# Block sums on VectorE, the first gate/up pair's weight operands kept in HBM, and the output stores spread over the last product

## Chip, core and metric

One NeuronCore of a Trainium2 chip runs the whole kernel. The metric is the device time of one execution in microseconds (us); the time before is the median of three executions.

## What is computed

A decoder layer over 1024 prompt tokens and 8 sample tokens, all fp32. The part that the change touches is its second half, and the gates ahead of it:

```python
h = rms_norm(x, norm1);  z = h @ w_in                # pool, q, k, v, ga, gb
merged = sigmoid(ga) * (y_pool @ w_pool_proj) + sigmoid(gb) * (y_attn @ w_attn_proj)
x = x + merged @ w_out
h2 = rms_norm(x, norm2)
x = x + (silu(h2 @ w_gate) * (h2 @ w_up)) @ w_down   # D_FF = 2816
```

## The kernel before

Every fp32 product is made of three fp32r products: each operand is split into a high part (a cast on ACT, line 138 for weights, 212 for activations) and the rest (a subtraction on DVE, lines 139 and 213), and PE adds high by high, high by rest and rest by high (`triple`, lines 1082 to 1086; `mm`, 207 to 209). All 1032 tokens are columns in two streams of 516, each of two halves of 258. A high part and a rest take a slot of the pools `whi` and `wlo` (4 slots each); raw weight blocks of 256 KB take one of 3 slots of `wraw`.

The stages in order of time, with the trace's times of before:

- attention and projections, to about 350 us;
- gates, 352 to 451: eight times `gate(1280, m)` with 72 matmuls, the first four followed by `mix(m)`;
- pool projection, 452 to 497;
- `out_proj(s, m)`, 497 to about 600: for stream s and block m 48 matmuls, the residual, a store of it to the HBM scratch `x2scr`, its square on ACT and a running sum of squares `acc` on POOL (line 969);
- for each stream `norm_scale` (the second RMS norm) and `combos`, which forms the seven left operands of a Strassen product from the four quarters of the normalized stream: four sums on POOL (lines 1011 to 1020), seven splits on ACT and DVE;
- gate and up products, about 597 to 1066: passes n = 0 to 11 over pairs p of 256 columns. Pass 0 is pair 0 for stream 0 alone, passes 1 to 10 are pairs 1 to 10 for both streams, pass 11 is pair 0 for stream 1. So stream 1 can still be normalized while pass 0 runs. `strassen` makes seven products for w_gate and seven for w_up; `wblocks` loads four quarters of a weight in two 512 KB transfers (`raw`), forms four differences on DVE (lines 1070 to 1078) and splits seven operands. Pair 0 is loaded and formed twice, in passes 0 and 11. A product is 12 matmuls where one stream runs and 24 where both do;
- `save` forms sums of a pass's result on POOL (line 1171, four per pass) and stores seven of them to HBM scratch (`s`);
- down products dx(1), dx(2), dy(6), dy(7), dy(4), dz(5), dz(3), 1066 to 1308. They read `ar` from that scratch and blocks `H` and `d` of w_down; `d`'s temporaries are slots of `wraw`. After dx(1), 12 additions `y` run on POOL. `residuals` loads 16 tiles `y` of 258 KB from `x2scr`;
- `store` (line 1293): five transposes on PE into one PSUM bank `po`, two copies on ACT (`ob` 128x512, `ys`), two or three transfers out. Sixteen of them; most are called where j == 3 of the last product.

The matmuls have one engine to themselves, PE. The order on each engine is made by a scheduler that models times, so it can move instructions across the order in which they are written. All transfers named here are issued by SP, one queue in order: a transfer that waits for a free slot holds all behind it.

Of the kernel before, what the change touches and what calls it, by code (L numbers as in the profile page):

```python
# [16 lines left out]
P = 128  # L17
# [19 lines left out]
def hybrid_step(tc, x_prompt, x_sample, cache_k, cache_v, state_pool, norm1, w_in, q_norm, k_norm, sinks,  # L37
# [860 lines left out]
    for what, m in ORDER:  # L898
        if what == "e":
            with tc.issue_after(live[15].yv.ins):  # L900
                pool_means(m)
        elif what == "g":
            attn_gate(m)
        elif what == "b":
            attn_proj(m)
    sg = []
    for m in range(8):
        sg.append(unit(u1, f"sg{m}"))
        gate(1280, m, sg[m])
        if m < 4:  # L910
            mix(m)
# [41 lines left out]
    def out_proj(s, m):  # L953
        ws = wload(wo_v, 0, 8, P * m)
        x2 = wide("x2")[:, :HT].rearrange("p (t c) -> p t c", t=2)
        xs = xscr[:, m].rearrange("p (t q c) -> p t q c", t=2, q=2)[:, :, s]
        SP.dma_start(x2, xs)
        ps = dbank("pw")
        for t in range(2):
            mm(ps[:, t, :NQ], ws, lambda k: (Mh[k][:, quarter(t, s)], Ml[k][:, quarter(t, s)]))  # L960
        V.tensor_add(x2, ps[:, :, :NQ], x2)
        SP.dma_start(x2scr[:, m, :, s], x2)
        if m == 0:
            A.activation(acc[s], x2, AF.Square)
        else:
            sq = t516("sq2").rearrange("p (t c) -> p t c", t=2)
            A.activation(sq, x2, AF.Square)  # L967
            if m < 7:
                G.tensor_add(acc[s], acc[s], sq)  # L969
            else:  # L970
                last[s] = sq
        A.activation(XG[s][:, :, m], x2, AF.Copy, scale=g2[m])
# [27 lines left out]
    def combos(s, out):  # L1000
# [10 lines left out]
        G.tensor_add(s1, a21, a22)  # L1011
        parts(1, a11)
        yield
        G.tensor_sub(s2, s1, a11)
        parts(2, a12)
        yield
        G.tensor_sub(a21, a11, a21)
        parts(6, s2)
        yield
        G.tensor_sub(a12, a12, s2)  # L1020
# [67 lines left out]
    def strassen(view, c0, streams, out):  # L1088

        sl = slice(streams[0], streams[-1] + 1)  # L1090
        ws = wblocks(view, c0)
# [73 lines left out]
    def save(p, g, sl):  # L1165
# [10 lines left out]
        comb(G.tensor_add, s1, a21, a22)  # L1176
        put(4, a22)
        put(5, s1)
        comb(G.tensor_sub, s2, s1, a11)
        put(6, s2)  # L1180
        comb(G.tensor_sub, a21, a11, a21)
        put(7, a21)
        put(2, a12)
        comb(G.tensor_sub, s4, a12, s2)
# [3 lines left out]
    norm = chain(norm_scale(1), combos(1, hc[1]))  # L1188
    for n, (p, streams) in enumerate([(0, [0])] + [(p, [0, 1]) for p in range(1, 11)] + [(0, [1])]):
        g = Gate()  # L1190
        u_ = Up(g)
        for i, _ in enumerate(chain(strassen(wg_v, 2 * P * p, streams, g), strassen(wu_v, 2 * P * p, streams, u_))):
# [33 lines left out]

    H1, H2 = {}, {}
# [7 lines left out]
    def operand(i, kk):  # L1235
# [3 lines left out]
        if i == 2:  # L1239
            return wd_row(k1, 0, wtemp("d21"))  # L1240
        if i == 6:
            w = wd_row(k0, 1, wtemp("d12"))
# [6 lines left out]
        if i == 4:  # L1249
            w = wd_row(k1, 0, wtemp("d21"))  # L1250
            V.tensor_sub(w, w, H1[kk])
            return w
        if i == 5:
            w = wtemp("t1")
# [38 lines left out]
    def store(f, t, y):  # L1293
# [10 lines left out]
        A.copy(o2[:n, :P], po[:n, 1, 0:P])  # L1304
# [15 lines left out]
    def residuals():  # L1320
        m1_es.close()
        mw_es.close()
        md, es = pool("md", bufs=20, side="right")
        mt[0] = md
        for t, m in ((0, 1), (1, 1), (1, 0), (0, 0)):
            Y[t, m] = residual(t, m)
# [31 lines left out]
    def stores(j, full=True):  # L1358
        for t, m, yy in ((0, 0, y11), (1, 0, y21), (1, 1, y22)) if full else ((0, 1, y12),):
            store(4 * m + j, t, yy[j])  # L1360

    for j in J:
        if j:
            stores(j - 1, False)
        if j == 2:
            stores(0)
        if j == 3:
            stores(1)
            stores(2)
            stores(3)  # L1370
        for kg in range(3):
# [7 lines left out]
            for k in range(n):  # L1379
                kk = 4 * kg + k  # L1380
                ah, al = a[kk]
                for s in range(2):
                    triple(z[j][:, s, :NQ], wh[:, k], wl[:, k], ah[:, s], al[:, s], False, kk == 10)
        V.tensor_add(y12[j], z[j][:, :, :NQ], y12[j])
    stores(3, False)
# [29 lines left out]
```

## Time and profile before

| | |
|---|---|
| median of 3 runs | 1323.27 us (1323.01 to 1325.38) |
| the profiled execution | 1322.94 us |
| its span in the trace | 1321.1 us |
| PE, PEld | 97%, 94% of the span |
| DVE, ACT, POOL | 63%, 38%, 15% |
| mean granted TensorE clock | 0.987 |
| HBM read, written | 105.10 MB, 34.48 MB |

The profile's page gives busy shares of the whole span. The trace behind it can be asked for single stretches: busy time by window, waits by engine, instructions by line and shape, the chain of work that ended last. A granted clock of 1.00 is the full 2.4 GHz, 0.50 the lower level; values between are stretches that hold both.

### The profile page before, as it was taken

The page shows a single profiled execution, that of the slowest core. Times are in us where ns is not written, and L with a number is a line of the kernel's source. Part 1 is how long each engine was busy: PE and PEld are TensorE (multiplying, and loading weights), DVE is VectorE, ACT ScalarE, POOL GpSimd, SP SyncE. Part 2 cuts the span into 40 slices and gives each one's busy share as a digit, 9 for nine tenths or more (in the row PEclk, how much of TensorE's full clock was granted, in tenths as well). Part 3 has the DMA queues.
Part 4 walks back from the last instruction along what each step waited for, and adds up shares of the span by engine and source line. Part 5 has one row for each costly group of instructions (what it writes and reads, how often), then busy time and mean ns, then how long its engine had stood idle before and what let it go on. Part 6 is the DMA issues. An engine that isn't in the chain of part 4 may idle for free.

```text
span 1321.1 us, 23770 instructions
## 1 busy us (share of the span) xinstructions
PE 1275.6 (97%) x9436; PEld 1243.5 (94%) x9436; DVE 838.8 (63%) x1519; ACT 507.8 (38%) x1003; POOL 195.1 (15%) x271
## 2 busy tenths in 40 slices
PE   7999999999999999987899999999999899899996
PEld 6998888999999999987899999999999899899996
DVE  6768667576233483499766567666666866766840
ACT  6555445442132234455323233222332343344423
POOL 3213200100000001152321022220122216000000
PEclk9999999999999999998899999999999999999998
DMA  7411101212111125643232222322323656855304
GB/s 243 136 35 41 41 21 44 77 36 57 41 49 48 49 81 156 173 126 106 77 121 77 93 97 98 121 89 81 113 81 121 209 192 217 263 182 194 121 9 121
DMA packets 139518, 139.86 MB, mean 106 GB/s; under 512 B 14391, under 2 KB 112375, under 8 KB 139383
## 3 DMA queue, kind: packets, MB, share of 16 engines
q1 hardware_dynamic: 139311, 137.08, 33.2%
q8 instruction: 74, 1.21, 0.4%
q0 software_dynamic: 96, 1.27, 0.2%
q14 instruction: 37, 0.30, 0.1%
HBM read 105.10 MB, written 34.48 MB: 106 GB/s over the span
## 4 chain that ended last, share of the span: by engine, by line
PE 89%; DVE 4%; DMA 3%; issue 2%; SPq 1%; ACT 1%; POOL 0%; DVEq 0%; ACTq 0%
PE pg L207 5%; PE pg L208 5%; PE pg L209 5%; PE py L1084 5%; PE py L1085 4%; PE py L1086 4%; PE pz L1086 3%; PE px L1084 3%; PE pz L1084 3%; PE px L1086 3%; PE pz L1085 3%; PE px L1085 3%; PE dy L1086 2%; PE dy L1084 2%; PE dy L1085 2%; PE pw L209 2%
## 5 line engine op out<-in xcount | busy, mean ns | idle before, releaser
L138 ACT CAST whi<-t 128x512 fp32r<-128x512 f32 x107 | 66.1, 621 | 174.9 <-PE py L1085 78.2
L207 PE MATMUL pg<-hTh,whi 128*128 128x384 f32 (+1 forms) x384 | 123.4, 322 | 0.0
L208 PE MATMUL pg<-hTl,whi 128*128 128x384 f32 (+1 forms) x384 | 123.1, 321 | 0.0
L209 PE MATMUL pg<-hTh,wlo 128*128 128x384 f32 (+1 forms) x384 | 122.7, 320 | 0.0
L139 DVE TENSOR_TENSOR wlo<-wraw,whi 128x512 fp32r<-128x512 f32 x95 | 70.2, 739 | 64.1 <-ACT whi L138 64.0
L138 ACT CAST whi<-wraw 128x512 fp32r<-128x512 f32 x95 | 58.8, 620 | 122.7 <-PE pa L208 31.3
L138 ACT CAST whi<-raw 128x512 fp32r<-128x512 f32 x72 | 44.5, 620 | 128.7 <-PE px L1085 49.0
L139 DVE TENSOR_TENSOR wlo<-t,whi 128x512 fp32r<-128x512 f32 x107 | 84.2, 789 | 14.6 <-ACT whi L138 14.3
L1171 POOL TENSOR_TENSOR fs<-g,g 128x516 f32<-128x516 f32 (+1 forms) x12 | 24.0, 2004 | 365.5 <-DVE g L1163 365.5
L209 PE MATMUL pw<-mh,wlo 128*128 128x258 f32 x256 | 73.1, 286 | 3.4 <-DVE wlo L139 3.4
L1084 PE MATMUL dy<-ah,whi 128*128 128x258 f32 x264 | 74.3, 284 | 0.6 <-DVE y L1339 0.6
L1085 PE MATMUL dy<-al,whi 128*128 128x258 f32 x264 | 74.0, 283 | 0.0
L212 ACT CAST ah<-ar 128x1032 fp32r<-128x1032 f32 (+1 forms) x42 | 41.3, 983 | 84.2 <-DMA ar<-s 77.9
L213 DVE TENSOR_TENSOR al<-ar,ah 128x1032 fp32r<-128x1032 f32 (+1 forms) x42 | 52.3, 1245 | 33.3 <-ACT ah L212 32.2
L207 PEld LDWEIGHTS pg<-hTh,whi 128*128 128x128 f32 x384 | 72.2, 188 | 1.1 <-DVE t L820 0.2
L207 PE MATMUL pw<-mh,whi 128*128 128x258 f32 x256 | 73.0, 285 | 0.0
L208 PEld LDWEIGHTS pg<-hTl,whi 128*128 128x128 f32 x384 | 72.2, 188 | 0.9
L208 PE MATMUL pw<-ml,whi 128*128 128x258 f32 x256 | 72.7, 284 | 0.0
L209 PEld LDWEIGHTS pg<-hTh,wlo 128*128 128x128 f32 x384 | 72.0, 188 | 0.4
L1086 PE MATMUL dy<-ah,wlo 128*128 128x258 f32 x264 | 72.0, 283 | 0.0
L969 POOL TENSOR_TENSOR acc<-acc,sq 128x516 f32<-128x516 f32 x12 | 17.4, 1446 | 315.1 <-ACT sq L967 315.1
L1084 PE MATMUL py<-c6h,whi 128*128 128x258 f32 x176 | 50.8, 289 | 6.2 <-DVE g L1160 6.2
(399 smaller groups left out, 4619.1 us busy)
## 6 DMA issues: line engine op xcount, KB each, us to landing
ar<-s SPq DMA_DIRECT2D x35, 516.0 KB
raw<-in_w_gate_dram SPq DMA_DIRECT2D x24, 512.0 KB
raw<-in_w_up_dram SPq DMA_DIRECT2D x24, 512.0 KB
s<-g SPq DMA_DIRECT2D x40, 258.0 KB
wraw<-in_w_in_dram SPq DMA_DIRECT2D x40, 256.0 KB
H<-in_w_down_dram SPq DMA_DIRECT2D x33, 256.0 KB
d<-in_w_down_dram SPq DMA_DIRECT2D x33, 256.0 KB
wraw<-in_w_out_dram SPq DMA_DIRECT2D x32, 256.0 KB
```

What stands on the lines that cost most here:

```text
L138: A.copy(hi, raw)
L139: e.tensor_sub(lo, raw, hi.bitcast(F32))
L207: T.matmul(ps, lhsT=wh, rhs=xh, start=(k == 0), stop=False)
L208: T.matmul(ps, lhsT=wh, rhs=xl, start=False, stop=False)
L209: T.matmul(ps, lhsT=wl, rhs=xh, start=False, stop=(k == n - 1))
L212: A.copy(hi, src)
L213: e.tensor_sub(lo, src, hi.bitcast(F32))
L969: G.tensor_add(acc[s], acc[s], sq)
L1084: T.matmul(ps, lhsT=wh, rhs=ah, start=start, stop=False, skip_group_check=True)
L1085: T.matmul(ps, lhsT=wh, rhs=al, start=False, stop=False, skip_group_check=True)
L1086: T.matmul(ps, lhsT=wl, rhs=ah, start=False, stop=stop, skip_group_check=True)
L1171: op(o[:, sl], a[:, sl], b[:, sl])
```

## The change

1. The running sums of squares (line 969), the sums in `combos` (1011 to 1020) and those in `save` (1171) move from POOL (`G`) to DVE (`V`): 12, 8 and 48 instructions.
2. `first_pair()` forms the 14 split operands of pair 0 during the gates, two per `gate` call for m = 0 to 6: 8 loads of 256 KB into `wraw`, 8 differences on DVE, 14 splits, and 28 stores of 256 KB to a new HBM scratch `wscr` (7.3 MB).
3. `kept()` gives those operands to passes 0 and 11: pass 0 reads 28 transfers of 256 KB straight into `whi`/`wlo` slots, pass 11 reads 14 of 512 KB into large units `wk`. Loads, differences and splits of pair 0 go from both passes (per pass 4 loads of 512 KB, 8 differences, 14 casts, 14 subtractions).
4. `dtemp`: the temporaries of w_down get four slots of their own (`wd`) in the pool `md`, which has 18 tiles in place of 20.
5. `store`: the copy `ys` goes from ACT to DVE; 15 of the 16 stores are called inside the last product, one after every second block for j = 1 to 3, and one is left for after it.

```diff
--- before.py
+++ after.py
@@ -903,10 +903,50 @@
             attn_gate(m)
         elif what == "b":
             attn_proj(m)
+
+    wscr = [scr.tile([P, 2, 4, P], F32, name=f"w{i}") for i in range(14)]
+
+    def first_pair():
+        for o, view in ((0, wg_v), (7, wu_v)):
+            def load(kh, m):
+                w = wraw()
+                SP.dma_start(w, view[:, 4 * kh:4 * kh + 4, P * m:P * m + P])
+                return w
+
+            def keep(i, w):
+                for a, part in enumerate(wsplit(w, 4)):
+                    SP.dma_start(wscr[o + i][:, a], part.bitcast(F32))
+
+            w = load(0, 0)
+            keep(0, w)
+            yield
+            b12 = load(0, 1)
+            V.tensor_sub(w, b12, w)
+            keep(4, w)
+            yield
+            b22 = load(1, 1)
+            keep(6, b22)
+            yield
+            V.tensor_sub(b12, b22, b12)
+            keep(3, b12)
+            yield
+            V.tensor_sub(w, b22, w)
+            keep(1, w)
+            yield
+            b21 = load(1, 0)
+            keep(2, b21)
+            yield
+            V.tensor_sub(w, b21, w)
+            keep(5, w)
+            yield
+
+    pre = first_pair()
     sg = []
     for m in range(8):
         sg.append(unit(u1, f"sg{m}"))
         gate(1280, m, sg[m])
+        for _ in range(2):
+            next(pre, None)
         if m < 4:
             mix(m)
     Mh, Ml = [], []
@@ -966,7 +1006,7 @@
             sq = t516("sq2").rearrange("p (t c) -> p t c", t=2)
             A.activation(sq, x2, AF.Square)
             if m < 7:
-                G.tensor_add(acc[s], acc[s], sq)
+                V.tensor_add(acc[s], acc[s], sq)
             else:
                 last[s] = sq
         A.activation(XG[s][:, :, m], x2, AF.Copy, scale=g2[m])
@@ -1008,16 +1048,16 @@
             out[i] = [x.rearrange("p (k c) -> p k c", k=4) for x in (hi, lo)]
 
         s1, s2 = unit(u1, "s1"), unit(u1, "s2")
-        G.tensor_add(s1, a21, a22)
+        V.tensor_add(s1, a21, a22)
         parts(1, a11)
         yield
-        G.tensor_sub(s2, s1, a11)
+        V.tensor_sub(s2, s1, a11)
         parts(2, a12)
         yield
-        G.tensor_sub(a21, a11, a21)
+        V.tensor_sub(a21, a11, a21)
         parts(6, s2)
         yield
-        G.tensor_sub(a12, a12, s2)
+        V.tensor_sub(a12, a12, s2)
         parts(7, a21)
         yield
         parts(5, s1)
@@ -1085,10 +1125,9 @@
         T.matmul(ps, lhsT=wh, rhs=al, start=False, stop=False, skip_group_check=True)
         T.matmul(ps, lhsT=wl, rhs=ah, start=False, stop=stop, skip_group_check=True)
 
-    def strassen(view, c0, streams, out):
+    def strassen(ws, streams, out):
 
         sl = slice(streams[0], streams[-1] + 1)
-        ws = wblocks(view, c0)
 
         def bank(name):
             return dbank(name)[:, sl, :NQ]
@@ -1173,23 +1212,38 @@
         a11, a12, a21, a22 = g[0, 0], g[0, 1], g[1, 0], g[1, 1]
         put(1, a11)
         s1, s2, s4 = half("fs1"), half("fs2"), half("fs4")
-        comb(G.tensor_add, s1, a21, a22)
+        comb(V.tensor_add, s1, a21, a22)
         put(4, a22)
         put(5, s1)
-        comb(G.tensor_sub, s2, s1, a11)
+        comb(V.tensor_sub, s2, s1, a11)
         put(6, s2)
-        comb(G.tensor_sub, a21, a11, a21)
+        comb(V.tensor_sub, a21, a11, a21)
         put(7, a21)
         put(2, a12)
-        comb(G.tensor_sub, s4, a12, s2)
+        comb(V.tensor_sub, s4, a12, s2)
         put(3, s4)
 
 
     norm = chain(norm_scale(1), combos(1, hc[1]))
+    def kept(o, in_units):
+
+        for i in range(7):
+            if in_units:
+                u = unit(u1, "wk", F32R)
+                SP.dma_start(u[:, :1024].bitcast(F32), wscr[o + i].rearrange("p a k c -> p (a k c)"))
+                u = u[:, :1024].rearrange("p (a k c) -> p a k c", a=2, k=4)
+                yield u[:, 0], u[:, 1]
+            else:
+                r = [wp.tile([P, 4, P], F32R, tag=t, bufs=4, name=t) for t in ("whi", "wlo")]
+                for a in range(2):
+                    SP.dma_start(r[a].bitcast(F32), wscr[o + i][:, a])
+                yield r
+
     for n, (p, streams) in enumerate([(0, [0])] + [(p, [0, 1]) for p in range(1, 11)] + [(0, [1])]):
         g = Gate()
         u_ = Up(g)
-        for i, _ in enumerate(chain(strassen(wg_v, 2 * P * p, streams, g), strassen(wu_v, 2 * P * p, streams, u_))):
+        for i, _ in enumerate(chain(strassen(wblocks(wg_v, 2 * P * p) if p else kept(0, n), streams, g),
+                                    strassen(wblocks(wu_v, 2 * P * p) if p else kept(7, n), streams, u_))):
             if n == 0 and i in (1, 4, 5, 6, 7, 8, 9, 10, 11):
                 next(norm)
         if n == 0:
@@ -1224,6 +1278,9 @@
         SP.dma_start(dst.rearrange("p j c -> p (j c)"), wd_v[:, f, 512 * m:512 * m + 512])
         return dst
 
+    def dtemp(name):
+        return Y["w"].tile([P, 4, P], F32, tag="wd", bufs=4, name=name)
+
     H1, H2 = {}, {}
 
     def keep(h, kk):
@@ -1237,9 +1294,9 @@
         if i == 1:
             return wd_row(k0, 0, keep(H1, kk))
         if i == 2:
-            return wd_row(k1, 0, wtemp("d21"))
+            return wd_row(k1, 0, dtemp("d21"))
         if i == 6:
-            w = wd_row(k0, 1, wtemp("d12"))
+            w = wd_row(k0, 1, dtemp("d12"))
             h2 = wd_row(k1, 1, keep(H2, kk))
             V.tensor_sub(h2, h2, w)
             V.tensor_add(H1[kk], H1[kk], h2)
@@ -1247,11 +1304,11 @@
         if i == 7:
             return H2[kk]
         if i == 4:
-            w = wd_row(k1, 0, wtemp("d21"))
+            w = wd_row(k1, 0, dtemp("d21"))
             V.tensor_sub(w, w, H1[kk])
             return w
         if i == 5:
-            w = wtemp("t1")
+            w = dtemp("t1")
             wd_row(k1, 1, H2[kk])
             V.tensor_sub(w, H2[kk], H1[kk])
             return w
@@ -1301,7 +1358,7 @@
         T.transpose(po[:n, 1, 0:P], y[:, small], ident)
         ob, o2 = t512("ob3"), t512("ys")
         A.copy(ob, po[:, 0])
-        A.copy(o2[:n, :P], po[:n, 1, 0:P])
+        V.tensor_copy(o2[:n, :P], po[:n, 1, 0:P])
         cols_ = slice(P * f, P * f + P)
         if t == 0:
             SP.dma_start(y_sample[:, 0, cols_], o2[:NS, :P])
@@ -1320,8 +1377,9 @@
     def residuals():
         m1_es.close()
         mw_es.close()
-        md, es = pool("md", bufs=20, side="right")
+        md, es = pool("md", bufs=18, side="right")
         mt[0] = md
+        Y["w"] = md
         for t, m in ((0, 1), (1, 1), (1, 0), (0, 0)):
             Y[t, m] = residual(t, m)
         Y["es"] = es
@@ -1355,19 +1413,14 @@
     for _ in srcs(3, a):
         pass
 
-    def stores(j, full=True):
-        for t, m, yy in ((0, 0, y11), (1, 0, y21), (1, 1, y22)) if full else ((0, 1, y12),):
-            store(4 * m + j, t, yy[j])
-
+    def full(j):
+        return [(4 * m + j, t, yy[j]) for t, m, yy in ((0, 0, y11), (1, 0, y21), (1, 1, y22))]
+
+    def part(j):
+        return [(4 + j, 0, y12[j])]
+
+    todo = full(0) + full(1) + part(0) + full(2) + part(1) + full(3) + part(2)
     for j in J:
-        if j:
-            stores(j - 1, False)
-        if j == 2:
-            stores(0)
-        if j == 3:
-            stores(1)
-            stores(2)
-            stores(3)
         for kg in range(3):
             n = min(4, 11 - 4 * kg)
             wh, wl = (wp.tile([P, 4, P], F32R, tag=t, bufs=4, name=t) for t in ("whi", "wlo"))
@@ -1381,8 +1434,10 @@
                 ah, al = a[kk]
                 for s in range(2):
                     triple(z[j][:, s, :NQ], wh[:, k], wl[:, k], ah[:, s], al[:, s], False, kk == 10)
+                if j and kk % 2:
+                    store(*todo.pop(0))
         V.tensor_add(y12[j], z[j][:, :, :NQ], y12[j])
-    stores(3, False)
+    store(*part(3)[0])
     flush()
     for e in (Y["es"], pd_es, u1_es, scr_es, tmp_es, wp_es, const_es):
         e.close()
```

The order that results, on SP. In the gates stage (before, where `wraw` are the raw slots):

```order
L692 DMA out_dram<-ob 8x128
L151 DMA wraw<-in_w_in_dram 128x4x128
L198 DMA wraw<-in_w_attn_proj_dram 64x4x128 x4
L151 DMA wraw<-in_w_in_dram 128x4x128 x16
L151 DMA wraw<-in_w_pool_proj_dram 128x4x128 x8
```

and now (`w_4181` and so on are the blocks of `wscr`):

```order
L151 DMA wraw<-in_w_in_dram 128x4x128 x2
L913 DMA wraw<-in_w_gate_dram 128x4x128 x2
L151 DMA wraw<-in_w_in_dram 128x4x128
L918 DMA w_4181<-whi 128x512
L918 DMA w_4181<-wlo 128x512
L918 DMA w_4185<-whi 128x512
L918 DMA w_4185<-wlo 128x512
L151 DMA wraw<-in_w_in_dram 128x4x128
L913 DMA wraw<-in_w_gate_dram 128x4x128
L918 DMA w_4187<-whi 128x512
L918 DMA w_4187<-wlo 128x512
L151 DMA wraw<-in_w_in_dram 128x4x128
```

The run of sixteen loads is broken up: loads of `w_in` now stand behind stores that wait for a cast on ACT or a subtraction on DVE.

From the last tiles of `out_proj` into pass 0, before:

```order
L1066 DMA raw<-in_w_gate_dram 128x4x256
L962 DMA x2scr<-x_6498 128x2x258
L1066 DMA raw<-in_w_gate_dram 128x4x256
L962 DMA x2scr<-x_6576 128x2x258
L1066 DMA raw<-in_w_up_dram 128x4x256 x2
L962 DMA x2scr<-x_6649 128x2x258
```

and now:

```order
L1106 DMA raw<-in_w_gate_dram 128x4x256
L1239 DMA whi<-w_4181 128x512
L1239 DMA wlo<-w_4181 128x512
L1239 DMA whi<-w_4182 128x512
L1239 DMA wlo<-w_4182 128x512
L1002 DMA x2scr<-x_6620 128x2x258
L1239 DMA whi<-w_4183 128x512
L1239 DMA wlo<-w_4183 128x512
L1106 DMA raw<-in_w_gate_dram 128x4x256
L1002 DMA x2scr<-x_6698 128x2x258
L1239 DMA whi<-w_4184 128x512
L1239 DMA wlo<-w_4184 128x512
```

The loads of pass 0 are now 28 transfers into `whi` and `wlo`, each waiting for PE to free a slot; raw blocks of pass 1 stand among them.

From the end of pass 11 into dx(1), before (`s` are sums stored by `save`, `y` the residual tiles; 14 more `y` rows follow the last):

```order
L1215 DMA ar<-s_0_5486 128x1032
L1168 DMA s_0_5504<-g_11720 128x258
L1224 DMA H<-in_w_down_dram 128x512 x2
L1215 DMA ar<-s_1_5493 128x1032
L1168 DMA s_0_5510<-fs_11971 128x258
L1168 DMA s_0_5516<-fs_11972 128x258
L1168 DMA s_0_5492<-g_11719 128x258
L1168 DMA s_0_5522<-g_11718 128x258
L1168 DMA s_0_5498<-fs_11973 128x258
L1215 DMA ar<-s_2_5494 128x1032
L1289 DMA y_12188<-x2scr 128x516
L1289 DMA y_12190<-x2scr 128x516
```

and now, where the last stores `s` of pass 11 are followed by one `H` and all 16 `y` rows, and these, behind the `y` rows, by:

```order
L1346 DMA y_12268<-x2scr 128x516
L1278 DMA H<-in_w_down_dram 128x512
L1269 DMA ar<-s_5_5613 128x516
L1278 DMA d_12462<-in_w_down_dram 128x512
L1278 DMA d_12492<-in_w_down_dram 128x512
L1278 DMA d_12528<-in_w_down_dram 128x512
L1278 DMA d_12558<-in_w_down_dram 128x512
L1278 DMA H<-in_w_down_dram 128x512
L1269 DMA ar<-s_0_5608 128x1032
```

Before, all `ar` and `H` of dx(1) (`ar<-s_0_5486` is its last `ar`) stood ahead of the `y` rows; now `ar<-s_5_5613`, `ar<-s_0_5608` and four `H` stand behind them, together with the first four `d` of dx(2).

## Rows read from the trace of the kernel before

**Rows 1.** Windows, core 0: columns as in the first row; x counts instructions.

```profile
core 0: us, PE busy (x) PEld busy (x) DVE busy (x) ACT busy (x) POOL busy (x), PEclk, DMA share, GB/s
352.00:451.00 99.00, 99.00 (x631) 99.00 (x630) 30.89 (x55) 27.04 (x53) 0.00 (x0) 1.00 0.15 44
580.00:650.00 70.00, 54.60 (x390) 52.56 (x389) 64.18 (x86) 33.30 (x53) 25.27 (x12) 0.88 0.33 98
1040.00:1070.00 30.00, 24.09 (x177) 23.67 (x177) 23.66 (x33) 12.22 (x22) 7.24 (x4) 0.89 0.49 156
1070.00:1120.00 50.00, 50.00 (x416) 49.93 (x416) 31.80 (x30) 19.73 (x30) 25.56 (x16) 1.00 0.67 227
1084.00:1096.00 12.00, 12.00 (x102) 12.00 (x101) 3.82 (x5) 4.03 (x6) 0.00 (x0) 1.00 1.04 388
1120.00:1150.00 30.00, 25.48 (x193) 24.66 (x192) 21.80 (x33) 7.91 (x12) 0.60 (x1) 0.94 0.80 263
1308.00:1321.10 13.10, 2.89 (x24) 2.14 (x22) 0.69 (x1) 4.60 (x12) 0.00 (x0) 0.72 0.49 139
```

**Rows 2.** Waits of PE, 560 to 700: total us, times, longest.

```profile
PE py L1084 <- DVE g L1160: 6.2, 1, 6.2
PE pz L1086 <- DVE wlo L139: 3.2, 1, 3.2
PE px L1084 <- ACT g L1107: 1.4, 1, 1.4
```

**Rows 3.** Instructions of DVE by form, 565 to 650: busy us, mean ns, idle before.

```profile
L139 DVE TENSOR_TENSOR wlo<-wraw,whi 128x512 fp32r<-128x512 f32 x6 | 9.0, 1504 | 0.0
L139 DVE TENSOR_TENSOR wlo<-raw,whi 128x512 fp32r<-128x512 f32 x10 | 8.8, 884 | 1.2 <-ACT whi L138 1.2
L1075 DVE TENSOR_TENSOR t<-raw 128x512 f32<-128x512 f32 x4 | 4.9, 1224 | 0.0
L213 DVE TENSOR_TENSOR c1l<-xg,c1h 128x1032 fp32r<-128x1032 f32 x2 | 6.0, 3004 | 0.0
L213 DVE TENSOR_TENSOR c2l<-xg,c2h 128x1032 fp32r<-128x1032 f32 x2 | 4.7, 2328 | 0.0
L213 DVE TENSOR_TENSOR c3l<-xg,c3h 128x1032 fp32r<-128x1032 f32 x2 | 2.4, 1224 | 0.0
```

**Rows 4.** Instructions of POOL by form, 565 to 650.

```profile
L1017 POOL TENSOR_TENSOR xg<-xg 128x1032 f32<-128x1032 f32 x2 | 6.2, 3108 | 0.0
```

**Rows 5.** Instructions of DVE by form, 690 to 900.

```profile
L139 DVE TENSOR_TENSOR wlo<-raw,whi 128x512 fp32r<-128x512 f32 x31 | 21.2, 683 | 2.5 <-ACT whi L138 2.5
L1147 DVE TENSOR_TENSOR g<-pz,g 128x516 f32<-128x516 f32 x11 | 7.6, 695 | 4.8 <-PE pz L1086 4.3
```

**Rows 6.** Chain that ended last, 575 to 592: start, us, what.

```profile
582.70 3.72 DMA raw<-in_w_gate_dram
```

**Rows 7.** Waits of PE, 1030 to 1160.

```profile
PE py L1084 <- DVE g L1111: 3.5, 1, 3.5
PE dx L1086 <- DVE wlo L139: 2.2, 1, 2.2
PE dx L1084 <- ACT whi L138: 1.8, 1, 1.8
```

**Rows 8.** Chain that ended last, 1110 to 1145.

```profile
1118.59 4.93 DMA ar<-s
1126.50 4.47 DMA d<-in_w_down_dram
```

**Rows 9.** Chain that ended last, 1295 to 1322.

```profile
1314.96 2.37 DMA out_dram<-ob
```

**Rows 10.** Timeline of ACT, 1299 to 1322: start, us, instruction, idle before.

```profile
1315.90 0.58 ACT L1303 COPY ob<-po 128x512 f32<-128x512 f32 x1 [0.17 <-DMA out_dram<-ys]
1317.35 0.25 ACT L1304 COPY ys<-po 8x128 f32<-8x128 f32 x1 [0.86 <-DMA out_dram<-ob]
```

**Rows 11.** Waits of SP's DMA queue, 352 to 451: total us, times, longest.

```profile
SPq L151 <- DVE wlo L139: 87.3, 14, 10.2
```

## The prediction

> **What bounds the kernel now.** I read the windows first [rows 1]. PE is busy all the time in most of the span (50.00 us of 50.00 from 1070 to 1120, 416 matmuls recorded), so a matmul costs 50.00/416 = 0.120 us there, and a change that keeps their number can only win where PE loses time. A stretch's loss is its length less its matmuls times 0.120; that counts idle time and time at a lower granted clock together.
>
> - 580 to 650 (end of out_proj, pass 0): 70 - 390 x 0.120 = **23.1 us**, at a granted clock of 0.88.
> - 1040 to 1070 (pass 11): 30 - 177 x 0.120 = 8.7 us.
> - 1120 to 1150 (dx(2) begins): 30 - 193 x 0.120 = 6.8 us.
> - 1308 to the end: 13.1 us, in which PE has 24 instructions (mostly transposes).
> - One wait near 687: 1.4 us [rows 2].
>
> Together 53 us; nothing else that PE shows can be won by this change.
>
> Who is late in the first stretch? The waits of PE name DVE: 6.2 us for `g` and 3.2 us for a weight's rest `wlo` [rows 2], and DVE is busy 64.18 of 70 us [rows 1]. By form its instructions are longer than elsewhere: a 128x512 subtraction takes 683 ns later on [rows 5], here 1504 ns for `wraw`, 884 for `raw`, 1224 for L1075; 128x1032 takes 3004 and 2328 ns for c1 and c2 against 1224 for c3 [rows 3]. The long ones lie beside POOL's block sums, at 3108 ns each [rows 4]. The excess in these rows is 6 x 0.82 + 10 x 0.20 + 4 x 0.54 + 2 x 1.78 + 2 x 1.10 = 14.8 us. Pass 0's raw loads come late as well: 3.72 us from issue to landing, on the chain that ended last [rows 6]. In pass 11 PE again waits for DVE, 3.5 us; dx(2) begins with 2.2 and 1.8 us for splits [rows 7], behind transfers `ar` (4.93 us) and `d` (4.47 us) [rows 8]. At the end the copies on ACT wait for earlier output transfers, 0.86 us before the last [rows 10], each 2.4 us or so [rows 9].
>
> **The transition (parts 1 to 3).** DVE loses the 14.8 us of excess and 22 weight instructions of 683 ns (15.0 us), and takes over 8 sums of 1.224 us (9.8), four `acc` sums of 0.695 (2.8) and four sums of pass 0 at half that size (1.4, an estimate from the same row): 15.8 us less work in a stretch where it had 64.18 of 70. ACT loses 14 casts. DVE then no longer sets the pace. Late next are the transfers: pass 0 now reads 28 x 0.262 = 7.3 MB in place of 2.1 MB of raw blocks. The stretch moved 98 GB/s x 70 us = 6.9 MB; it would be 12.1 MB. The best rate of queued 258 KB transfers is 388 GB/s from 1084 to 1096 [rows 1]: the 7.3 MB take 19 us, against 14 x 12 x 0.120 = 20.2 us of matmuls. That is balanced, if the queue runs without gaps; but each of these transfers waits for a `whi` or `wlo` slot, four of each, that PE frees, and raw blocks of pass 1 stand among them. The other end: if each product's pair lands as the raw block did, 3.72 us for 512 KB, and one after the other, pass 0 takes 52 us, of which some 10 can be filled with products of pass 1: 22 us lost, as much as before. So the loss afterwards lies between 0 and 22 us. I take 9, nearer the queued rate, since four slots allow several transfers in flight: **gain 14** (1 to 23). The wait of 1.4 us at 687 stood behind a sum on POOL that takes 0.695 us on DVE: gain 1.4.
>
> The Trainium skill ("SBUF — State Buffer", section The DMA setup-cost knee) says a transfer pays about 2 us whatever its size, gives 224 GB/s at 256 KiB, and asks for the largest transfers. By that figure, as an estimate, the 28 loads take 33 us, some 13 us more than the matmuls, and the gain would be 10, the time 1302. The window at 388 GB/s, with sixteen 258 KB transfers behind each other, speaks against it; where slots leave only one in flight it would hold, and its time lies between the forecast and the first rival.
>
> **Pass 11 and dx(1), dx(2) (parts 1, 3, 4).** The weight work and POOL's sums go; 14 loads of 512 KB are asked for early in the queue, during pass 10, where the DMA had spare time, so they should be there. Of 8.7 us I take 5. What takes its place: the 16 `y` transfers (4.2 MB, 11 us at 388 GB/s) now stand ahead of `ar` 5, `ar` 0 and four `H` of dx(1). A block of dx(1) is 24 matmuls, 2.9 us; the eighth is due 20 us after dx(1) begins and the first `H` behind the burst should land at about 15 us, the last `ar` shortly before its block at 25 us. So it fits with 2 to 5 us to spare; if not, 3 to 7 us are lost. For dx(2), `d` is loaded earlier and has four slots of its own: 0 to 5 of the 6.8 us come back. Both together: +1. Sum of this part: **gain 6** (-3 to 13).
>
> **Gates (part 2).** PE is busy 99.00 of 99.00 us [rows 1], so nothing can be gained. Added: 22 DVE instructions (15 us on 30.89), 14 casts (9 on 27.04 of ACT), 36 transfers (9.4 MB, 95 GB/s on 44). All three have room. SP's queue stood 87.3 us waiting for slots [rows 11]; now loads of the gates stand behind stores that wait for a split, at most 0.6 + 0.7 = 1.3 us, and a slot stays taken until its store has read it. A gate takes 99/8 = 12.4 us; its load and split, 3.72 + 1.3 = 5.0 us by the raw block, can be 7 us late before PE waits. I take **a loss of 1** (0 to 9; the upper end is 1.3 us for each of seven gates, if a load, a split, a store and a second load with its split follow one another: 5.0 + 3.7 + 5.0 = 13.7 against 12.4).
>
> **The end (part 5).** After the last matmul there remains one sum (0.7), five transposes (5 x 0.12), `ob` and `ys` (0.6, 0.25) [rows 10], a transfer (2.4) [rows 9] and the issues between: 5.5 us in place of 13.1. But 19 transposes now lie ahead of the last matmul, 2.3 us. **Gain 5** (2 to 7). The other stores hide beside dz(3): five for each j of 66 x 0.120 = 7.9 us, 1.3 MB, 167 GB/s. ACT and DVE were below half busy; if a copy that waits for an output slot holds the next cast, up to 3 us go.
>
> **Sum.** 14 + 1.4 + 6 - 1 + 5 = 25.4 us. The profiled execution took 1322.94 us (span 1321.1), 0.3 below the median of 1323.27: 1322.94 - 25.4 = 1297.5, as a median **1298 us**.
>
> **Rivals.**
> - *Pass 0 waits for transfers* (0.20). The loads cannot run ahead, since PE frees the slots that they need; the 52 us case. For it: in-order queue, four slots, 1.2 to 1.8 times the former bytes. Against: 388 GB/s when queued. The transition gains nothing, the rest stands: 1322.9 - 11.4 = **1312**.
> - *All comes back* (0.13). Transfers run as in the burst, pass 11 and dx(2) have no waits: 23 + 1.4 + 8.7 + 3 + 5 = 41, so **1282** to 1288.
> - *The gates starve: slower* (0.09). Each kept operand holds its slot for a landing L, a split of 1.3 and a landing of its store, and two follow one another within each gate on the same slots: 2 x (2L + 1.3) against 12.4 us. It decides from L = 2.45 us on; output transfers land in 2.37 [rows 9], the raw block in 3.72 [rows 6]. At 3.72 it costs 17.5 - 12.4 = 5 us in seven gates, 35 us in all: 1323 - 25 + 35 = **1333**. Against: three raw and four split slots, so that two in series is the worst order.
> - *DVE stays late* (0.06). The sums on DVE stand ahead of `g` and `wlo` in its in-order queue, and stream 1's normalization, which stays, holds PE in pass 0; the end gains 5, the gates lose some: **1320**.
>
> **Chances and range.** The forecast (1289 to 1306) has 0.52. The range 1285 to 1313 adds most of the transfer case and part of the full recovery. About 0.2%, 2.6 us, can be told from no change: faster 0.86, same 0.05, slower 0.09.
>
> **What would show it.** Right: 580 to 650 with DVE well below 64 us and no 128x512 subtraction over 0.8 us there; PE's waits there name DMA `whi` or `wlo`; PE at 100% from 352 to 451; about 6 us after the last dz matmul. Wrong: waits of PE for `wlo` of a gate before 451; a wait for `ar` or `H` late in dx(1), near 1070 to 1100; waits for `g` on DVE in pass 0; granted clock still below 0.9 in the transition; casts on ACT waiting behind `ob` in the last product.

## The result and the profile after

The changed kernel takes 1308.67 us (median of 4 runs, 1307.47 to 1311.92), before 1323.80 (4 runs beside it): ratio 0.9888, 95% interval 0.9867 to 0.9909. It is faster by 15 us, where 25 were forecast. The profiled execution took 1308.06 us, span 1306.3.

The windows of the changed kernel, with the columns of [rows 1]:

```profile
core 0: us, PE busy (x) PEld busy (x) DVE busy (x) ACT busy (x) POOL busy (x), PEclk, DMA share, GB/s
250.00:260.00 10.00, 10.00 (x55) 9.52 (x55) 3.54 (x15) 3.01 (x15) 0.00 (x0) 0.83 0.23 90
359.60:453.20 93.60, 93.60 (x590) 93.35 (x589) 41.12 (x72) 34.00 (x66) 0.00 (x0) 1.00 0.44 141
585.00:655.00 70.00, 63.74 (x498) 61.15 (x497) 52.10 (x86) 27.01 (x41) 0.00 (x0) 0.98 0.56 180
700.00:800.00 100.00, 100.00 (x835) 100.00 (x834) 63.75 (x102) 27.96 (x47) 0.00 (x0) 1.00 0.32 102
1040.00:1070.00 30.00, 30.00 (x253) 30.00 (x252) 16.02 (x28) 9.62 (x14) 0.00 (x0) 1.00 0.76 243
1070.00:1085.00 15.00, 9.47 (x64) 9.26 (x64) 3.48 (x5) 4.42 (x7) 0.00 (x0) 0.77 0.96 363
1125.00:1160.00 35.00, 31.44 (x237) 30.09 (x237) 28.59 (x43) 11.82 (x17) 0.00 (x0) 0.95 0.71 232
1298.40:1306.30 7.90, 1.01 (x8) 0.55 (x6) 1.44 (x4) 1.17 (x2) 0.00 (x0) 0.83 0.46 134
```

In the gates PE is busy all the time, in the transition (the end of out_proj and pass 0) 64 of 70 us, and pass 11 has no gap. But there is a hole from 1070 to 1085, in dx(1), where the kernel before had none: PE is busy 9.47 of 15 us, with the DMA at 0.96 of its time and the granted clock at 0.77 (part of the stretch at the lower level, 1.2 GHz). Waits of PE over the whole span, six of the rows that lie in the part that the change touches:

```profile
PE dx L1124 <- ACT whi L138: 5.5, 1, 5.5
PE po L1357 <- DVE y L1439: 2.4, 1, 2.4
PE py L1124 <- DVE g L1150: 2.1, 1, 2.1
PE py L1124 <- DVE g L1156: 1.7, 1, 1.7
PE px L1124 <- ACT g L1146: 1.1, 1, 1.1
PE py L1126 <- DMA wlo<-w: 0.5, 1, 0.5
```

The first two are new at this size: before, the longest wait of `dx` for `whi` was 1.8 us [rows 7]. Of the old ones `g` L1160 (6.2) and `wlo` (3.2) [rows 2] are gone.

To compare kernels I count a stretch's loss as in the prediction, its length less its matmuls times 100.00/835 = 0.1198 us (the row from 700 to 800). The stretches are fixed to the kernel's own events, since the same work begins at another time in each kernel. The transition is 60 to 150 us after the first matmul of out_proj; "next" is the 80 us after it; "pass 11" goes from 500 us after that matmul to the first of dx; then come the first 40 us of dx and the 80 us after those. "End" is the time from the last dz matmul to the span's end. Each row is one profiled execution, in us; e1 to e12 are the experiments of the next sections.

| kernel | transition | next | pass 11 | dx, first 40 | dx, 80 more | end | median of runs |
|---|---|---|---|---|---|---|---|
| before | 23.4 | 2.3 | 9.0 | 0.0 | 7.1 | 13.0 | 1323.80 |
| the change | 10.7 | 1.1 | -0.1 | 7.3 | 8.6 | 7.9 | 1308.67 |
| e1 y late | 11.9 | 1.0 | -0.2 | 7.4 | 15.8 | 7.6 | 1311.41 |
| e2 ys on ACT | 13.2 | 1.0 | -0.2 | 6.8 | 9.2 | 6.6 | 1307.16 |
| e3 sums only | 17.8 | 1.1 | 5.9 | -0.1 | 6.7 | 12.4 | 1312.70 |
| e4 pass 11 in slots | 11.4 | 1.1 | 6.2 | 0.5 | 7.2 | 7.9 | 1309.11 |
| e5 half in units | 9.9 | 1.1 | -0.2 | 4.2 | 11.1 | 7.8 | 1306.58 |
| e6 sums on POOL | 17.1 | 1.2 | -0.1 | 12.2 | 11.7 | 8.6 | 1321.82 |
| e7 y on DVE | 11.0 | 1.1 | -0.1 | 6.8 | 6.1 | 7.8 | 1302.99 (one run) |
| e8 pass 0 only | 13.0 | 1.1 | 8.0 | -0.2 | 6.2 | 9.2 | 1308.38 |
| e9 half the loads | 10.5 | 1.0 | -0.1 | 6.6 | 8.2 | 8.4 | 1305.27 (one run) |
| e10 y and ys | 11.2 | 1.1 | -0.2 | 6.5 | 5.6 | 6.5 | 1304.35 |
| e11 y spread | 10.8 | 1.1 | -0.2 | 3.7 | 5.3 | 6.5 | 1304.69 |
| e12 y spread, half | 12.5 | 1.1 | -0.1 | 5.2 | 3.4 | 6.6 | 1301.35 |

So the change won 12.7 us in the transition and 9.1 in pass 11, and gave 8.8 back in dx. Executions of one kernel scatter by 2 to 9 us, so below a few us a stretch's loss says more than a median. It scatters too: nine kernels besides the change (e1, e2, e4, e5, e7, e8 and e10 to e12) run the same code in the transition, and with it they lose 9.9 to 13.2 us there, so a difference under some 3 us in that column says nothing. The rows of the transition, first before, then the change:

```profile
555.90:645.90 90.00, 74.60 (x556) 72.63 (x555) 83.11 (x101) 43.26 (x66) 38.93 (x16) 0.91 0.35 106
```

```profile
558.50:648.50 90.00, 83.74 (x662) 81.03 (x661) 71.15 (x107) 40.15 (x60) 0.00 (x0) 0.98 0.59 183
```

### The profile page after: what moved, and what is told of

Read it like the earlier page. It is cut to its first block, busy times and chain, and to the rows that moved or that the text cites. A ratio compares the mean times of both kernels' runs of the same rounds, so it can differ in the third digit from the quotient of the medians.

```text
span 1306.3 us, 23839 instructions
## 1 busy us (share of the span) xinstructions
PE 1272.9 (97%) x9436; PEld 1239.5 (95%) x9436; DVE 813.3 (62%) x1581; ACT 496.3 (38%) x973; POOL 72.9 (6%) x203
## 4 chain that ended last, share of the span: by engine, by line
PE 89%; DMA 5%; DVE 2%; SPq 1%; issue 1%; ACT 1%; DVEq 0%; ACTq 0%
PE pg L207 5%; PE pg L208 5%; PE pg L209 5%; PE py L1124 5%; PE py L1126 5%; PE py L1125 5%; PE pz L1124 3%; PE px L1126 3%; PE px L1124 3%; PE pz L1125 3%; PE pz L1126 3%; PE px L1125 3%; PE pw L207 2%; PE pw L208 2%; PE pw L209 2%; PE dy L1126 2%
## 5 line engine op out<-in xcount | busy, mean ns | idle before, releaser
L139 DVE TENSOR_TENSOR wlo<-wraw,whi 128x512 fp32r<-128x512 f32 x109 | 74.8, 687 | 80.3 <-ACT whi L138 71.5
L138 ACT CAST whi<-wraw 128x512 fp32r<-128x512 f32 x109 | 67.1, 620 | 142.4 <-PE pa L208 31.3
L138 ACT CAST whi<-t 128x512 fp32r<-128x512 f32 x91 | 56.1, 621 | 166.3 <-PE py L1125 82.7
L138 ACT CAST whi<-raw 128x512 fp32r<-128x512 f32 x60 | 37.2, 621 | 113.8 <-PE px L1125 62.8
L139 DVE TENSOR_TENSOR wlo<-t,whi 128x512 fp32r<-128x512 f32 x91 | 61.7, 684 | 11.5 <-ACT whi L138 11.4
L1394 POOL TENSOR_TENSOR y<-y,ds 128x516 f32<-128x516 f32 x12 | 20.4, 1733 | 841.7 <-DVE wlo L139 841.7
L139 DVE TENSOR_TENSOR wlo<-raw,whi 128x512 fp32r<-128x512 f32 x60 | 41.0, 684 | 30.3 <-ACT whi L138 30.3
L1124 PE MATMUL dx<-ah,whi 128*128 128x258 f32 x176 | 50.1, 289 | 5.5 <-ACT whi L138 5.5
```

The costliest lines, as they stand in the source:

```text
L138: A.copy(hi, raw)
L139: e.tensor_sub(lo, raw, hi.bitcast(F32))
L1124: T.matmul(ps, lhsT=wh, rhs=ah, start=start, stop=False, skip_group_check=True)
L1394: G.tensor_add(y[j], y[j], s1)
```

## Experiments on the transition

Each expectation names a theory and its rivals. Ratios are to runs of the kernel before that were taken beside the experiment.

**e3, the sums alone.** The kernel before with every `G.` of part 1 made `V.`, no other edit:

```diff
-                G.tensor_add(acc[s], acc[s], sq)
+                V.tensor_add(acc[s], acc[s], sq)
...
-        comb(G.tensor_add, s1, a21, a22)
+        comb(V.tensor_add, s1, a21, a22)
```

> The kernel before with the 68 block sums and sums of squares on DVE and nothing else of the change. Theory (POOL's sums stretched DVE's subtractions by some 15 us around 565 to 650, and that was more than half of the loss there): from out_proj's start to dx's start 10 to 13 us less than before's 573.4, time about 1311. Rival (DVE stays late with its weight work, and PE's loss stays): 2 to 5 us less, time 1318 to 1321. Second rival (the sums now stand ahead of g and wlo on DVE): no gain, 1323 or more.

Measured: 1312.70 us, ratio 0.9920 (0.9897 to 0.9943). From out_proj to dx it takes 563.5 us against 573.4, which is the theory at its lower edge. The long subtractions of [rows 3] are gone. By form on DVE in e3, 565 to 650:

```profile
L139 DVE TENSOR_TENSOR wlo<-wraw,whi 128x512 fp32r<-128x512 f32 x6 | 4.1, 691 | 0.0
L139 DVE TENSOR_TENSOR wlo<-raw,whi 128x512 fp32r<-128x512 f32 x11 | 7.5, 686 | 0.0
L213 DVE TENSOR_TENSOR c1l<-xg,c1h 128x1032 fp32r<-128x1032 f32 x2 | 2.5, 1225 | 0.0
```

The subtraction of 1504 ns became 691, that of 3004 became 1225. Over the whole span DVE does 68 instructions more than before (1587 against 1519) and is busy less, 821.9 us against 838.8. Some two thirds of the whole gain come from moving 68 small instructions. In the transition itself, though, it is only 5.6 us of 12.7: PE then waits for the rest of a weight (`pz` for DVE's `wlo`, 5.3 us at the longest in e3).

**e6, the rest without the sums.** The changed kernel with part 1 undone: the 68 instructions go back to POOL.

> The changed kernel with the 68 block sums and sums of squares back on POOL; all else of the change stands. The loss in the transition (from 60 us after out_proj's start to 150 after it) was 23.4 us before, 17.8 with the sums alone on DVE, 10.7 with the whole change. Theory (two causes that add up: POOL's sums stretch DVE, and the weight work of pass 0 fills it): 23.4 - (17.8 - 10.7) = 16 us lost, 15 to 18; pass 11 loses 1 to 3 us; time 1313 to 1318. Rival (either of them alone frees DVE, so that the other one is nearly free): transition 10 to 13 us, time 1308 to 1311.

Measured: 1321.82 us (10 runs), ratio 0.9970 (0.9950 to 0.9990). The transition loses 17.1 us, as the theory had it, and the subtraction of `wraw` there takes 1504 ns again. Either part alone gives about 6 us (23.4 to 17.8, 23.4 to 17.1) and both 12.7, so within the scatter they add up. Pass 11 lost nothing, less than expected: operands read into `wk` need no work on DVE. The time is later than the theory and the rival said, because dx loses 24 us; without the sums, the rest of the change is hardly worth having. Its longest wait of PE:

```profile
PE dx L1124 <- ACT whi L138: 9.8, 1, 9.8
```

**e9, half the transfers of pass 0.** It leaves out the weights' rests in pass 0 and uses the high parts in their place.

```diff
-                r = [wp.tile([P, 4, P], F32R, tag=t, bufs=4, name=t) for t in ("whi", "wlo")]
-                for a in range(2):
-                    SP.dma_start(r[a].bitcast(F32), wscr[o + i][:, a])
-                yield r
+                r = wp.tile([P, 4, P], F32R, tag="whi", bufs=4, name="whi")
+                SP.dma_start(r.bitcast(F32), wscr[o + i][:, 0])
+                yield r, r
```

> The changed kernel, where pass 0 reads only the high parts of its kept operands and uses them in place of the rests too: 14 transfers of 256 KB in place of 28; the correction by the weights' rests is left out there, with as many matmuls. It tells what of the 10.7 us still lost in the transition is the transfers' doing. Theory (pass 0 is paced by its loads, and pass 1's raw blocks come late behind them, so that DVE waits 2.7 us for one with a sum for PE behind it): 5 to 7 us lost. Rival (stream 1's normalization and sums fill DVE from 608 to 637 us, and PE waits for that): 9 to 11 us.

Measured: 1305.27 us in one run, and 10.5 us lost in the transition against 10.7. That is the rival: over the whole transition the transfers do not set the loss. The windows from 608 to 638 us, first the changed kernel, then e9 (whose out_proj began 1.8 us earlier):

```profile
608.00:638.00 30.00, 26.00 (x199) 24.33 (x199) 29.22 (x41) 13.36 (x20) 0.00 (x0) 1.00 0.56 181
```

```profile
608.00:638.00 30.00, 24.65 (x185) 23.53 (x184) 27.52 (x39) 13.01 (x18) 0.00 (x0) 0.96 0.34 100
```

The rate fell from 181 to 100 GB/s and PE did no more; DVE stayed nearly full (27.52 of 30).

Inside the transition the transfers do show, which the sum hides. In the changed kernel the chain that ended last lies mostly on the loads until 613 us, two of them being

```profile
600.21 5.38 DMA wlo<-w
607.43 5.96 DMA wlo<-w
```

and from 617.8 to 636.9 on DVE almost alone. In e9 it lies on DVE already from 606.7 to 635. By loss, from 100 to 120 us after out_proj's start 4.0 us in the changed kernel became 1.6 in e9, and the 20 us after that lost 6.1 in place of 4.2. So with fewer loads PE came through the first part sooner and then waited longer for DVE. While the loads ran, the DMA moved 347 GB/s from 598.5 to 608.5 and 328 from there to 618.5, not far from the 388 GB/s that the prediction took.

Of the other waits of PE there, one began with a transfer. The changed kernel's timeline on DVE, with the idle time before an instruction and what ended it:

```profile
603.52 0.69 DVE L1110 TENSOR_TENSOR t<-raw 128x512 f32<-128x512 f32 x1 [2.74 <-DMA raw<-in_w_up_dram]
604.13 0.15 DVE L119 TENSOR_TENSOR rs_a<-rstd 86x6 f32<-86x6 f32 x1
604.20 0.42 DVE L1156 TENSOR_TENSOR g<-py,g 128x258 f32<-128x258 f32 x1
```

A difference for pass 1 (L1110) waits 2.74 us for its raw block, and the sum that PE waits for (`g` L1156, 1.7 us) stands behind it in DVE's queue.

## Experiments on pass 11 and dx

What makes the hole at 1070? In the changed kernel ACT's cast of an `H`, a block of w_down, waits 14 us for its transfer:

```profile
1077.16 0.62 ACT L138 CAST whi<-H 128x512 fp32r<-128x512 f32 x1 [13.99 <-DMA H<-in_w_down_dram]
```

On SP's queue the 16 `y` rows went out ahead of it:

```profile
1058.02 0.39 SPq L1278 DMA_DIRECT2D H<-in_w_down_dram  x1
1061.91 9.40 SPq L1346 DMA_DIRECT2D y<-x2scr  x16
1071.67 0.33 SPq L1278 DMA_DIRECT2D H<-in_w_down_dram  x1
```

**e1, y later.**

```diff
-            if mid and kk == KKS[5]:
+            if mid and kk == KKS[10]:
```

> One edit to the changed kernel: the 16 loads of the residual tiles y are called at the end of dx(1)'s blocks and not in their middle, so on SP's queue they stand behind all ar and H of dx(1). Theory (the y burst ahead of ar and H makes the new stall of dx(1), 7.3 us lost between 1070 and 1085): that stall goes, less than 2 us are lost there, time about 1302 (1300 to 1304). Rival (ar and H are late anyway, because the units wk of pass 11 hold the slots that they need until PE has read them): at least 4 us are still lost in dx(1), time 1306 to 1309. Second rival (y then comes late for the additions on POOL and for dy): the loss moves to 1120 to 1160, time about 1308.

Measured: 1311.41 us, ratio 0.9912 (0.9881 to 0.9943); 7.4 us are lost in the first 40 us and 15.8 in the next 80. Both rivals came true together. On SP nine of the eleven `H` now precede the end of the `y` rows, but the last two were issued behind all of them, at 1076.4, and cast at 1083.1 (9.87 us after ACT's previous work, for `DMA H`); `ar` of dx(2) and the copies for the `y` sums came late too. So a later call alone does not help. It does not acquit the order: two `H` still stand behind the burst.

**e4, pass 11 through slots.**

```diff
-... if p else kept(0, n), streams, g),
+... if p else kept(0, 0), streams, g),
-... if p else kept(7, n), streams, u_))):
+... if p else kept(7, 0), streams, u_))):
```

> One edit to the changed kernel: pass 11 reads its kept operands through the whi and wlo slots, as pass 0 does, and not into units wk; the scheduler then puts ar and H of dx(1) ahead of the y burst, as before the change. Theory (the units wk took the room in which ar and H were loaded early, and so brought the y burst ahead of them): the stall of 7.3 us in dx(1) goes. What pass 11 then loses by loading at the pace of PE's slots: 2 to 6 us. Time 1303 to 1308. Rival (the stall comes from the DMA being full whatever the order): dx(1) still loses 5 us or more, time 1310 to 1314.

Measured: 1309.11 us, 0.9895 (0.9866 to 0.9924). The hole is gone (0.5 us) and pass 11 loses 6.2: PE waits there for `DMA whi<-w`, 3.2 us in three waits. So the units `wk` bring the hole about: `ar`, `H` and `wk` are all units of one pool of 28, and a unit that holds a `wk` is free for dx(1) only when PE has read it. How they do it shows on SP's queue in all fourteen profiles. Where all eleven `H` of dx(1) stand ahead of `y` (before, e3, e4, e8) the first 40 us of dx lose at most 0.5 us; in the other ten kernels three to five `H` stand behind the first `y` rows, and 3.7 to 12.2 us are lost. No kernel keeps `wk` in units and has all `H` ahead of `y`, so whether the place in the queue alone costs the time stays open. The time was 1 us above the theory's window, since what is won in dx is lost in pass 11.

**e5, seven operands in units, seven in slots** (`kept(7, n)` to `kept(7, 0)`).

> One edit to the changed kernel: in pass 11 the seven operands of w_gate are read into units wk as before, the seven of w_up through whi and wlo slots. On SP's queue five of the six ar and eight of the eleven H of dx(1) then stand ahead of the y burst, where the changed kernel has four and seven. Theory (the units wk hold the room of the early ar and H, and all of pass 11 in slots lost 6.2 us to the slots' pace): in the first 40 us of dx(1) at most 2 us are lost in place of 7.3, and in pass 11 up to 3 us in place of none; sum 27.5 less 3 to 6, time 1303 to 1306. Rival (the DMA has no room there: what one stretch gains the next one loses): sum of losses within 2 us of 27.5, time 1307 to 1310.

Measured: 1306.58 us, 0.9871 (0.9845 to 0.9896). Pass 11 loses nothing and the first 40 us of dx 4.2, but the next 80 us lose 11.1 in place of 8.6. From the transition to the last dz matmul, stretches between those of the table included, the losses sum to 27.1 us against 27.5. That is the rival: the loss moves. The median is 2 us lower, within the scatter.

**e8, kept operands for pass 0 only** (`if p else kept(0, n)` to `if p or n else kept(0, n)`, likewise for 7).

> The changed kernel, where pass 11 loads, forms and splits pair 0 anew as before the change; pass 0 still reads it from scratch. Theory (kept operands gain in pass 0, and pass 11's gain is paid back in dx(1)): transition 10 to 12 us lost, pass 11 5 to 7 (5.9 with the sums alone), the first 40 us of dx(1) under 1; sum within 2 us of the changed kernel's 27.5, time 1307 to 1310. Rival (the units of pass 11 pay): 3 us or more slower than the changed kernel, 1312 or more.

Measured: 1308.38 us, 0.9880 (0.9854 to 0.9907). The transition and pass 11 lose 13.0 and 8.0 us, each 1 us more than the theory had, and dx loses about what it did before the change. There is no net difference to the changed kernel, so for pass 11 the kept operands gained nothing in sum.

**e7, the additions y on DVE.**

```diff
-            G.tensor_add(y[j], y[j], s1)
+            V.tensor_add(y[j], y[j], s1)
```

> The changed kernel with the 12 additions y after dx(1) on DVE too. They run on POOL beside DVE's splits of dx(2) (al 1.7 to 2.3 us in place of 1.23) and PE waited 1.5 us for one. Theory: the wait for al goes, the loss from 40 to 120 us after dx(1)'s start falls from 8.6 to 6 or 7; 12 x 0.69 = 8.3 us are added to DVE. Rival (that stretch loses time to transfers of d and H, not to DVE): 8 to 10 us as now. Second rival (12 sums ahead of the splits in DVE's queue): 10 us or more.

Measured: 1302.99 us in one run; the 80 us lose 6.1 in place of 8.6, as the theory said. The splits beside these additions, in the changed kernel from 1090 to 1112:

```profile
L213 DVE TENSOR_TENSOR al<-ar,ah 128x1032 fp32r<-128x1032 f32 x3 | 5.5, 1842 | 3.8 <-ACT ah L212 3.8
```

and in e7, 1088 to 1110, with the additions:

```profile
L1394 DVE TENSOR_TENSOR y<-y,ds 128x516 f32<-128x516 f32 x12 | 7.5, 690 | 0.0
L213 DVE TENSOR_TENSOR al<-ar,ah 128x1032 fp32r<-128x1032 f32 x4 | 4.9, 1228 | 2.6 <-ACT ah L212 2.6
```

## Experiments on the end, and a faster version

**e2, ys back on ACT.**

```diff
-        V.tensor_copy(o2[:n, :P], po[:n, 1, 0:P])
+        A.copy(o2[:n, :P], po[:n, 1, 0:P])
```

> One edit to the changed kernel: the copy ys goes back from DVE to ACT. Theory (ys waits on DVE for an output transfer to free its slot, and the last sum y12 stands behind it in DVE's queue: PE's last transposes wait 2.4 us for it): the wait goes, from the last dz matmul to the end 5.5 to 6 us in place of 7.9, time about 1306.5. Rival (the same wait then stands in ACT's queue ahead of the next ob and the casts): no change within 1 us, or PE waits for whi in the last product, time 1308 to 1310.

Measured: 1307.16 us, 0.9874 (0.9847 to 0.9900); the end 6.6 us in place of 7.9, and PE's wait for `y` L1439 0.9 in place of 2.4. That is the theory, with 1.3 us and not 2; all other kernels with `ys` on DVE have 7.6 to 9.2 us there. In the changed kernel DVE has at the end:

```profile
1298.63 0.28 DVE L1361 COPY ys<-po 4x128 f32<-4x128 f32 x1 [1.43 <-DMA out_dram<-ys]
1300.01 0.28 DVE L1361 COPY ys<-po 8x128 f32<-8x128 f32 x1 [1.10 <-DMA out_dram<-ob]
1300.22 0.67 DVE L1439 TENSOR_TENSOR y<-dz,y 128x516 f32<-128x516 f32 x1
```

The last sum, whose operand was ready at about 1298.7, stands behind a copy that waits for an output transfer.

**e10, both edits (e7 and e2).**

> The changed kernel with two edits that gained alone: the 12 additions y on DVE, the copy ys on ACT. Theory (they lie in different stretches and add up): losses 24.8 as with y on DVE, the end 6.6 us in place of 7.8 to 7.9; time 1301 to 1303. Rival (single runs scatter by 4 us and the gains were in the scatter): 1305 to 1309.

Measured: 1304.35 us, 0.9851 (0.9831 to 0.9871). In the profile both gains are there: the 80 us of dx lose 5.6, the end takes 6.5. The median lies between the theory's time and the rival's.

**e11, y in four groups**, with e10's edits:

```diff
-    down(1, x, True, True, residuals)
+    down(1, x, True, True, {KKS[5]: residuals, KKS[8]: later(1, 1), KKS[10]: later(1, 0)})
...
-    down(2, x, False, True)
+    down(2, x, False, True, {KKS[3]: later(0, 0)})
```

> The same two edits, and the 16 loads of y in four groups of four, called in the middle, after the ninth and after the eleventh block of dx(1) and after the fourth of dx(2). Theory (4.2 MB of y in one piece are what H waits for): under 3 us lost in the first 40 us of dx(1) in place of 6.8, and no more after it; 1297 to 1300. Rival (the DMA is full there in any order, 391 GB/s, and what H gains d and ar lose, as with the late burst): sum of losses in dx as in the run with y in one piece, within 2 us.

Measured: 1304.69 us, 0.9855 (0.9839 to 0.9872), but 1299.64 in the profiled run, the lowest of the four: 3.7 us are lost in the first 40 us in place of 6.5, and no more after. The stretch moved the way that the theory said, about half as far as it takes to remove the loss; the median did not move.

**e12, e11 and e5 together.**

> The last one, with the seven operands of w_up in pass 11 read through whi and wlo slots, so that five of six ar and eight of eleven H stand ahead of y. Theory (room in the units and the piece of y both hold H back): under 2 us lost in the first 40 us of dx(1), 6 to 8 in the rest of dx; 1295 to 1299. Rival (the transfers only move the loss): 1301 to 1304.

Measured: 1301.35 us (1300.43 to 1302.55), 0.9827 (0.9812 to 0.9842). That is 7 us below the changed kernel, and the intervals do not touch. The time is the rival's. Against e11 the gain is not clear of the noise: the median is 3 us lower, but e11's profiled run was quicker than any of e12, and dx loses 8.6 us in e12's profile, 9.0 in e11's. The loss moved: the rest of dx falls (5.3 to 3.4) and the first 40 us rise (3.7 to 5.2), where the theory had under 2. What is left of PE's waits from dx to dz:

```profile
PE dx L1124 <- ACT whi L138: 3.5, 1, 3.5
PE dx L1125 <- DVE al L213: 2.0, 1, 2.0
PE dy L1126 <- DVE wlo L139: 0.4, 1, 0.4
```

## Why the prediction was right and where it failed

The direction held and the time lies in the range, outside the forecast's own 1289 to 1306; the gain was 15 us and not 25. That the time is not at the range's edge is luck: pass 11 won 4 us more than its term, without which it would have been about 1313, while dx came out 10 us worse than its term. Term by term, profile against profile:

- **Transition, gain 14: measured 12.7.** The size was right, and so was the cause on DVE (stretched subtractions and weight work, e3 and e6). The steps "DVE then no longer sets the pace" and "late next are the transfers" were wrong. The loads hold the chain only at first, and halving them left the loss where it was (e9). I took 15.8 us of work off DVE; its busy time in the transition fell by 12.0 (83.11 to 71.15 of 90 us), and from 608 to 638 us it was still full (29.22 of 30), with stream 1's normalization, its splits and pass 1's weights. That was the last rival's mechanism, at a lower price. So the size was in part luck, being reached with another limit than the one that I priced. The transfer rival, which had 0.20, would have left the transition its 23 us; it lost 10.7. That DVE now sets the pace is read from its windows and the chains, and from e9; it was not tried by taking DVE work away.
- **The wait at 687, gain 1.4:** it is still 1.1 us long (`px` for `g` L1146). So POOL's sum was not all that it waited for. The stretch around it gained 1.2.
- **Pass 11, 5: measured 9.1.** The term was undersized; the `wk` were there in time.
- **dx, +1: measured -8.8**, 7.3 in the first 40 us and 1.5 in the next 80. This is the step that made the difference between 25 and 15: "the first `H` behind the burst should land at about 15 us". I let the burst begin with dx(1). dx(1) began at 1049.1, but the burst stood behind the last stores `s` of pass 11 and went out at 1061.9, after waiting 3.4 us for one of them; the `H` behind it went out at 1071.7 and was cast at 1077.2, 28 us after dx(1)'s start. And I took the new order as given; it comes with the units that `wk` holds (e4), which I never counted.
- **Gates, -1: measured -0.2** (93.4 us from the first to the last gate result before, 93.6 now). The rival of starved gates was far off.
- **The end, 5: measured 3.4** (the last product 1.7 us longer by its transposes, the end 13.0 to 7.9). I priced a copy that holds what stands behind it on ACT, and not on DVE, where `ys` had gone and where the last sum stands (e2).
- **Not in the sum:** the gates began 2.3 us later, at 359.6 in place of 357.3, in code that the change does not touch. One piece is the row 250 to 260, granted clock 0.83, where before it was 1.00. In the other profiles of changed kernels the gates began at 357.1 to 359.3, so this is scatter.

12.7 + 1.2 + 9.1 - 8.8 - 0.2 + 3.4 - 2.3 = 15.1 us; the spans differ by 14.8. Of the signs that I had named, those for being right came for DVE (no 128x512 subtraction over 0.8 us, the gates at 100%), and two for being wrong came as well: waits for `g` on DVE in pass 0 and a wait for `H` in dx(1).

The Trainium skill ("SBUF — State Buffer", section The DMA setup-cost knee) says that every transfer pays a fixed cost and asks for fewer and larger ones. Here half as many, with half the bytes, were worth 0.2 us, within the scatter, since something else ended last; so no run here tests that rule. The Trainium skill ("SBUF — State Buffer", section Who interferes with whom) also says that a DVE instruction with two inputs in SBUF contends with a POOL instruction that reads SBUF. The traces agree: with POOL's part gone, 3004 ns became 1225 in e3 and 1842 became 1228 in e7.

## What to carry to other kernels

That POOL was idle did not make small sums on it free: they cost DVE more than DVE needed to do them itself (e3). Ask first what an idle engine slows down. A buffer that is filled early takes its room from whatever was filled early before; when a pool is shared, look for the loads that now wait for a release, and where they stand in the queue. And before calling a resource "late next", price its rival at the same place: here DVE still had 29 of 30 us to do.

## What the runs showed of the hardware

- POOL's additions `y` took 1733 ns each (12, busy 20.4 us in all in the changed kernel), and the splits beside them on DVE 1842 ns; on DVE (e7) the additions took 690 ns, and the splits 1228. DVE was busy 7.5 us with the twelve additions, and the 80 us of dx lost 2.5 us less.
- Two sources of delay on one engine, POOL's sums and pass 0's weight work on DVE, added up in PE's loss (5.6 and 6.3 us alone, 12.7 together, in a column that scatters by 3).
